# Decay matmuls on 128 partitions, every mask added on TensorE, and the y sum of the scan by one reduction over three planes

## The chip, the cores and the metric

The kernel runs on 1 core of one Trainium2 chip. The metric is the device time of one execution in microseconds (us), the median of the runs shown. Engine names as in the profile: PE is TensorE's matmul, PEld its weight load, DVE is VectorE, ACT ScalarE, POOL GpSimd, SP the engine whose queue issues every DMA of this kernel.

## The reference, cut to what matters

One step of a two-layer trunk over 256 context and 1024 latent tokens, width 1024. Layer one is attention beside a convolution. Layer two, which the change is about, is a bidirectional scan: 32 heads of 64 channels, 4 groups that share B and C, a state of 128, chunks of 128 tokens.

```python
a_cum = jnp.cumsum(dtc * a_neg.reshape(G, E), axis=2)
seg = a_cum[:, :, :, None] - a_cum[:, :, None, :]
decay = jnp.exp(jnp.where(causal, seg, -jnp.inf))
cb = jnp.einsum('bclgn,bcsgn->bclsg', cf, bf)
y_diag = jnp.einsum('bclsg,bclsge,bcsgep->bclgep', cb, decay, xdt)
...
y_off = jnp.einsum('bclgn,bcgepn,bclge->bclgep', cf, prev, jnp.exp(a_cum))
y = (y_diag + y_off).reshape(b, L, G, E, P)
...
y = y_f + jnp.flip(y_b, 1) + d_skip.reshape(SSD_GROUPS, SSD_HPG, 1) * xs
y = rmsnorm(y.reshape(b, L, SSD_INNER) * jax.nn.silu(z), g_norm)
```

## The kernel before, in words

Everything is held transposed, channels on the partitions and tokens along the row. Large products are done as three matmuls (`mm3`, lines 119 to 121: high by high, high by low, low by high part, in `F32R`), each moving 512 or 256 columns.

Layer two goes in 8 units `u` of 4 heads. For each unit the loop over the 10 chunks `c` of 128 tokens runs `scan_a(u, c + 1)` (one chunk ahead), then `scan_b(u, c)`, then `advance`, which carries the forward state. Between them a scheduler, which orders each engine's instructions ahead of time, lays the matmuls and convolutions of the next unit's input blocks (`conv_block`, `z_block`: lines 119 to 121 into `psmm`, line 848 on DVE), so that TensorE has long runs of dense matmuls around the scan's small ones. In the last unit, u = 7, no input blocks of a next unit are left.

`scan_a` makes the decay matrices of 4 heads and both directions (`dr`). A decay exponent is a difference of two running sums, one by row and one by column, and it is made by one matmul over 10 rows per direction: rows 0 and 1 of a group multiply ones by the high and low part of the one sum (tile `mv`, 4 heads by 128 columns), rows 2 to 9 multiply the other sum's parts (tile `lt`) by rows of `mv` that are one for one head and zero elsewhere. Direction 0 lies on partitions 0 to 9 and direction 1 on partitions 32 to 41 of the same two tiles (line 1136). Then the causal mask, 0 or -1e30, has to be added before the exponential. In the units below `MU = 6` DVE adds it (line 1141) and ACT takes the exponential of the sum in SBUF (line 1142). In units 6 and 7 a bf16 matmul of an identity with the mask adds it in PSUM (line 1144), and ACT reads PSUM (line 1145). POOL adds the two directions (line 1152) and DVE multiplies by `cb` (line 1153).

`scan_b` makes the output y of a chunk: `po` (line 1165) is the part of the states that come in, for one or both directions, and DVE multiplies it in place by the factors `eb`, planes [j, direction, t] (line 1174). `pd` (line 1170) is the part inside the chunk. Then DVE adds `pd` and the D term `xdv` (line 1178), adds the plane of each direction (line 1180, twice where there are two), and multiplies by the gate (line 1181). In chunks 0 and 1 only one direction has a state, so 8 of a unit's 10 chunks have two.

`load_m` brings 2 rows of `mv` and 8 of `lt` per direction (lines 1113 and 1114), two buffers each; `load_x` brings `xa`, 1024 columns of the array `cmb` (B, x, C, D term, gate), and the two halves of `eb`. All stand in SP's one queue.

Of the kernel before, what the change touches and what calls it, by code (L numbers as in the profile page):

```python
# [10 lines left out]
F32 = mybir.dt.float32  # L11
F32R = mybir.dt.float32r
I32 = mybir.dt.int32
BF16 = mybir.dt.bfloat16
AF = mybir.ActivationFunctionType
ALU = mybir.AluOpType
AX = mybir.AxisListType
# [39 lines left out]
def _body(nc, tc, d, es, dbg, stop):  # L57
    V, S, G, PE = nc.vector, nc.scalar, nc.gpsimd, nc.tensor
    dma = nc.sync.dma_start
# [11 lines left out]
    def f32(ap):  # L71
        return ap.bitcast(F32)
# [23 lines left out]
    ident = cp.tile([128, 128], F32, name="ident")  # L96
# [111 lines left out]
    sel = cp.tile([128, 2], F32, name="sel")  # L208
# [67 lines left out]
    def row(name="row", n=T, parts=128, dt=F32):  # L276
        return rows.tile([parts, n], dt, name=name, tag="row")
# [153 lines left out]
    fold = att.tile([64, 64], F32, name="fold", bufs=1)  # L431
    dma(fold, d["fold"])
    for c0, n in CHUNKS:
        ps = psum()
# [18 lines left out]
    for i in range(2):  # L453
        wh, wl = split_w(d["wa"][9 + i], 8, 128)
        s = row("qsq")
# [65 lines left out]
    for c0, n in CHUNKS:  # L521
        ps = bcast_cols(rq, c0 // 128, n // 128, ps=psum("pt"))
# [177 lines left out]
    for i in range(len(units) + 2):  # L700
        if i < len(units):
            u = units[i]
# [102 lines left out]
    cc = pool("cc", side="right", stack=esC)  # L805
# [11 lines left out]
    identb = cc.tile([128, 128], BF16, name="identb")  # L817
    V.tensor_copy(identb, ident)
    maskb = cc.tile([128, 2, 128], BF16, name="maskb")
    NMV, MU = 2, 6  # L820
    dec_bc = cc.tile([128, 128, 5], F32, name="dec_bc")
    dte = cc.tile([128, NCH, 2, NH], F32, name="dte")

    cmb = dp.tile([8, NCH, 128, 1408], F32, name="cmb")
    yzd = dp.tile([16, 128, T], F32, name="yzd")
    mvd = dp.tile([NCH, 2, 2, NH, 128], F32, name="mvd")
    ltd = dp.tile([NCH, 2, NH, 2, 128], F32, name="ltd")
# [30 lines left out]
        lin(wh, wl, 8, 128, h_h, h_l, CHUNKS, cb)  # L858
        return conv_post(blk, raw)

    OB, OX, OCT, OXD, OSZ, OBT = 0, 128, 384, 512, 768, 1024

    def z_part(blk, tz, w=None):
        wh, wl = w or split_w(d["wc"][blk], 8, 128)
# [48 lines left out]
    cr = pool("crow", bufs=4, side="left", stack=esK)  # L913
    maskU = cr.tile([128, 128], F32, name="maskU", tag="row")
    maskL = cr.tile([128, 128], F32, name="maskL", tag="row")
# [13 lines left out]
    w = dtile("w")  # L929
    S.activation(w, z, AF.Square)  # L930
    p = dtile("p")
# [43 lines left out]
    for half in range(2):  # L975
        hs = slice(half * 64, half * 64 + 64)
        for c0 in range(0, 5):
            c = half * 5 + c0
            ps = psum("sd")
# [20 lines left out]
            dma(eyd[half * 5:half * 5 + 5, :, dr].rearrange("c r t -> r c t"),  # L1000
                ey[r0:r0 + 32, :].rearrange("r (c t) -> r c t", t=Q))
    mvs, lts = [], []
    cts = [cr.tile([64, w], F32, name=n, tag="row") for n, w in (("mvc", 512), ("ltc", 128))]
    for t, n in zip(cts, ("mvc", "ltc")):
        dma(t, d[n])
    for i in range(NMV):
        mv = cc.tile([64, 512], F32R, name=f"mv{i}")
        lt = cc.tile([64, 128], F32R, name=f"lt{i}")
        S.copy(mv, cts[0])
        S.copy(lt, cts[1])  # L1010
        mvs.append(mv)
        lts.append(lt)
    dump("al", al)
# [43 lines left out]
    sp = pool("ssd", bufs=2, side="right", stack=esC)  # L1057
# [50 lines left out]
    xas, ebs, cbs, bts = {}, {}, {}, {}  # L1108

    def load_m(u, c):  # L1110
        mv, lt = mvs[c % NMV], lts[c % NMV]
        for dr in range(2):
            dma(f32(mv[32 * dr:32 * dr + 2]), mvd[c, dr, :, 4 * u:4 * u + 4].rearrange("x h t -> x (h t)"))
            dma(f32(lt[32 * dr + 2:32 * dr + 10]), ltd[c, dr, 4 * u:4 * u + 4].rearrange("h x t -> (h x) t"))

    def load_x(u, c):
        xa = xas[c] = sp.tile([128, 1024], F32, name="xa", tag="xa", bufs=3)
        dma(xa, cmb[u, c, :, 0:1024])
        if u % 2 == 0:
            bts[c] = sp.tile([128, 128], F32, name="bt", tag="bt")  # L1120
            dma(bts[c], cmb[u, c, :, OBT:OBT + 128])
        eb = ebs[c] = sp.tile([128, 2, 2, 128], F32, name="eb", tag="eb")
        for pr_ in range(2):
            ev = eyd[c, 4 * u:4 * u + 4].rearrange("(j p) d t -> p j (d t)", p=2)[pr_]
            dma(eb[pr_ * 64:pr_ * 64 + 64].rearrange("p j d t -> p j (d t)"),
                ev.unsqueeze(0).to_broadcast([64, 2, 256]))

    def scan_a(u, c):
        xa = xas[c]
        ct = xa[:, OCT:OCT + 128]  # L1130
        mv, lt = mvs[c % NMV], lts[c % NMV]
        pss = [psum("sd") for _ in range(2)]
        es_ = [sp.tile([128, 4, 128], F32, name="et", tag="et", bufs=4) for _ in range(2)]
        for dr, ps in enumerate(pss):
            r = slice(32 * dr, 32 * dr + 10)
            PE.matmul(ps, lt[r], mv[r], start=True, stop=u < MU)  # L1136
        for dr, ps in enumerate(pss):
            et = es_[dr].rearrange("p h t -> p (h t)")
            p3, mk = ps.rearrange("p (h t) -> p h t", h=4), maskb[:, dr:dr + 1].to_broadcast([128, 4, 128])
            if u < MU:  # L1140
                V.tensor_add(es_[dr], p3, mk)
                S.activation(et, et, AF.Exp)  # L1142
            else:
                PE.matmul(p3, identb, mk, start=False, stop=True)
                S.activation(et, ps, AF.Exp)
        if u % 2 == 0:
            pc_ = psum("sd")
            PE.matmul(pc_[:, :128], bts[c], ct, start=True, stop=True)
            cbs[c] = sp.tile([128, 128], F32, name="cb", tag="cb", bufs=NCH)
            S.copy(cbs[c], pc_[:, :128])  # L1150
        mt = es_[0]
        G.tensor_add(mt, es_[0], es_[1])  # L1152
        V.tensor_mul(mt, mt, cbs[c].unsqueeze(1).to_broadcast([128, 4, 128]))
        return xa, mt

    def scan_b(u, c, prev, st, y):
        xa, mt = st
        xt, ct = xa[:, OX:OX + 256], xa[:, OCT:OCT + 128]
        xdv, szv = xa[:, OXD:OXD + 256], xa[:, OSZ:OSZ + 256]
        eb = ebs[c]  # L1160
        dirs = [dr for dr in range(2) if prev[dr] is not None]
        po = psum("sd")
        for dr in dirs:
            for pi in range(2):
                PE.matmul(po[:, dr * 256 + pi * 128:dr * 256 + (pi + 1) * 128],  # L1165
                          prev[dr][:, pi * 128:(pi + 1) * 128], ct, start=True, stop=True)
        pd = psum("tm" if u == 7 else "sd")
        for j in range(4):
            b, pi = (j % 2) * 64, j // 2
            PE.matmul(pd[b:b + 64, pi * 128:(pi + 1) * 128], xt[:, j * 64:(j + 1) * 64], mt[:, j, :],  # L1170
                      start=True, stop=True)
        d0, d1 = dirs[0], dirs[-1] + 1
        yo = eb[:, :, d0:d1].rearrange("p j d t -> p d j t")
        V.tensor_mul(yo, po[:, d0 * 256:d1 * 256].rearrange("p (d j t) -> p d j t", j=2, t=128), yo)

        def v2(ap):
            return ap.rearrange("p (a t) -> p a t", a=2)
        V.tensor_add(y, v2(pd[:, :256]), v2(xdv))
        for dr in dirs:
            V.tensor_add(y, y, eb[:, :, dr])  # L1180
        V.tensor_mul(y, y, v2(szv))
        sq, ac = eb[:, :, d0], ysq[:, c * Q:c * Q + Q]
        S.activation(sq, y, AF.Square)
        if u:
            G.tensor_add(sq[:, 0], sq[:, 0], sq[:, 1])
            G.tensor_add(ac, ac, sq[:, 0])
        else:
            G.tensor_add(ac, sq[:, 0], sq[:, 1])
# [32 lines left out]
    for u in range(8):  # L1221
# [24 lines left out]
        for c in range(NCH):  # L1246
# [7 lines left out]
            if u < 7:  # L1254
                y = sp.tile([128, 2, 128], F32, name="yz", tag="yz")
            else:
                y = ylast[c // 5][:, :, (c % 5) * Q:(c % 5 + 1) * Q]
# [10 lines left out]
            elif c % 5 == 4:  # L1268
                f = c // 5
# [130 lines left out]
def _tables():  # L1400
    rows_ = TS // GRID_W
    f = np.float32
    r = np.repeat(np.arange(rows_, dtype=f), GRID_W)
    c = np.tile(np.arange(GRID_W, dtype=f), rows_)
    inv = np.power(f(10000.0), -np.arange(8, dtype=f) / f(8)).astype(f)
    ang = np.concatenate([r[:, None] * inv, c[:, None] * inv], axis=-1).astype(f)
    cos, sin = np.cos(ang).astype(f), np.sin(ang).astype(f)
    tab = np.zeros((128, T), f)
    tab[:96] = 1.0
    for i in range(32):  # L1410
        tab[64 + i, TP:] = cos[:, i // 2]
        tab[96 + i, TP:] = -sin[:, i // 2] if i % 2 == 0 else sin[:, i // 2]
    ident = np.eye(128, dtype=f)
    fold = np.zeros((64, 64), f)
    for i in range(64):
        for j in range(64):
            if i % 32 == j % 32:
                fold[i, j] = 1.0
    s, l = np.meshgrid(np.arange(128), np.arange(128), indexing="ij")
    maskU = (l >= s).astype(f)  # L1420
    maskL = (l <= s).astype(f)
    mvc = np.zeros((2, 32, 4, 128), f)
    ltc = np.zeros((2, 32, 128), f)
    ltc[:, 0:2] = 1.0
    for r in range(8):
        mvc[:, 2 + r, r // 2, :] = 1.0
    tab = np.stack([tab, np.concatenate([tab[64:], tab[:64]])])
    sel = np.zeros((128, 2), f)
    for i in range(128):
        if i % 32 < 2:  # L1430
            sel[i, i % 32] = 1.0
    return dict(sel=sel, tab=tab, ident=ident, fold=fold, maskU=maskU, maskL=maskL, mvc=mvc.reshape(64, 512), ltc=ltc.reshape(64, 128))


def _kblk(w):
# [107 lines left out]
```

## Time and profile before

| | |
|---|---|
| median of 3 runs | 2105.81 us (2104.4 to 2105.97) |
| profiled execution | 2106.15 us, of which the span from its first to its last instruction is 2104.3 us |
| busy in the span | PE 2024.6 us (96%), PEld 1627.3, DVE 1488.0 (71%), ACT 885.2 (42%), POOL 700.4 (33%) |
| mean granted TensorE clock | 0.981 |

Matmuls are pipelined: the duration of a matmul in the trace reaches past the start of the next one, and its end is modelled. What a matmul costs a busy PE is therefore read from the distance between two starts, and not from its duration, and PE may count as busy while it waits for weights. The scans of layer two lie from about 1090 us (the first decay matmul starts at 1093.8 us) to about 1895 us.

### The profile page before, as it was taken

Reading aid. Unit: us, or ns where it says so; the run is one execution under the profiler, and the core shown is the slowest. Engines: PE = TensorE matmul, PEld = TensorE weight load, DVE = VectorE, ACT = ScalarE, POOL = GpSimd, SP = SyncE. Lnnn points to the kernel's source line nnn. Section 1 sums busy time; section 2 is a strip of 40 time slices with the busy share of each in tenths; the row PEclk is TensorE's granted clock in tenths of the full one; section 3 lists DMA queues with packets and bytes.
Section 4 is the critical chain, followed back from the end, with each engine's and each line's share of the span. In section 5 each row is a group of like instructions: output and inputs, shape, how many; then the busy total and the mean of one; then the engine's idle time right before and its main releaser. Section 6 shows DMA issues by size and latency. Waiting matters only on the chain.

```text
span 2104.3 us, 32156 instructions
## 1 busy us (share of the span) xinstructions
PE 2024.6 (96%) x11710; PEld 1627.3 (77%) x11710; DVE 1488.0 (71%) x2361; ACT 885.2 (42%) x1683; POOL 700.4 (33%) x567
## 2 busy tenths in 40 slices
PE   6999999999999999989999999999999999899997
PEld 4777888677767768878887777778777777579997
DVE  5797897666666673457669797977898596873743
ACT  5411312566566672334544333343344333334531
POOL 1211112213141303543135354545454454662001
PEclk9999999999999999999999999999999999999998
DMA  8424123221112126222667657755765578655442
GB/s 331 165 105 147 53 103 121 63 75 43 54 46 76 51 83 220 108 86 76 176 205 220 207 176 211 215 169 187 222 198 181 166 218 252 215 173 191 143 154 70
DMA packets 251453, 313.32 MB, mean 149 GB/s; under 512 B 19904, under 2 KB 200096, under 8 KB 251296
## 3 DMA queue, kind: packets, MB, share of 16 engines
q1 hardware_dynamic: 251296, 311.28, 46.3%
q8 instruction: 93, 1.52, 0.3%
q14 instruction: 64, 0.52, 0.1%
HBM read 223.15 MB, written 88.05 MB: 148 GB/s over the span
## 4 chain that ended last, share of the span: by engine, by line
PE 79%; DVE 8%; DMA 4%; issue 3%; POOL 3%; ACT 1%; SPq 1%; DVEq 0%; POOLq 0%; ACTq 0%
PE psmm L119 16%; PE psmm L120 16%; PE psmm L121 16%; PE pspo L666 5%; PE pspt L646 4%; PE pss L119 3%; PE pssd L1078 2%; PE pss L120 2%; PE pss L121 2%; PE pssd L1165 2%; PE pssd L1136 2%; PE pssd L1170 1%; PE psx L229 1%; DVE cy L848 1%; DMA eb<-eyd 1%
## 5 line engine op out<-in xcount | busy, mean ns | idle before, releaser
L119 PE MATMUL psmm<-hl,wh 128*128 128x512 f32 (+1 forms) x1152 | 425.8, 370 | 7.0 <-ACT wh L114 3.5
L121 PE MATMUL psmm<-hl,wl 128*128 128x512 f32 (+1 forms) x1152 | 425.8, 370 | 4.0 <-POOL wl L115 4.0
L120 PE MATMUL psmm<-hl,wh 128*128 128x512 f32 (+1 forms) x1152 | 424.8, 369 | 0.0
L115 POOL TENSOR_TENSOR wl<-ws,wh 128x1024 fp32r<-128x1024 f32 x89 | 226.2, 2543 | 473.6 <-ACT wh L114 394.5
L119 PEld LDWEIGHTS psmm<-hl,wh 128*128 128x128 f32 x1152 | 222.6, 193 | 47.2 <-issue 9.5
L121 PEld LDWEIGHTS psmm<-hl,wl 128*128 128x128 f32 x1152 | 222.3, 193 | 41.0 <-issue 6.6
L120 PEld LDWEIGHTS psmm<-hl,wh 128*128 128x128 f32 x1152 | 222.7, 193 | 36.9 <-issue 8.3
L383 DVE SCALAR_TENSOR_TENSOR cacc<-cvin,acw,cacc 128x1295 f32<-128x1295 f32 x120 | 207.0, 1741 | 4.6 <-ACT cacc L378 3.1
L114 ACT CAST wh<-ws 128x1024 fp32r<-128x1024 f32 x109 | 113.5, 1042 | 196.1 <-PE psmm L120 136.7
L848 DVE SCALAR_TENSOR_TENSOR cy<-raw,prm,cy 128x1282 f32<-128x1282 f32 x96 | 164.8, 1717 | 20.8 <-ACT cy L845 19.7
L120 PE MATMUL psmm<-hlo,wh 128*128 128x512 f32 (+3 forms) x480 | 171.5, 358 | 0.1
L121 PE MATMUL psmm<-hh,wl 128*128 128x512 f32 (+3 forms) x480 | 169.3, 356 | 0.0
L119 PE MATMUL psmm<-hh,wh 128*128 128x512 f32 (+3 forms) x480 | 167.6, 359 | 1.6 <-ACT hh L259 1.6
L617 DVE TENSOR_REDUCE mx<-pss 128x1 f32<-128x512 f32 (+1 forms) x208 | 137.3, 668 | 35.4 <-PE pss L121 34.6
L1152 POOL TENSOR_TENSOR et<-et 128x512 f32<-128x512 f32 x80 | 118.9, 1486 | 104.9 <-ACT et L1142 75.7
L120 PE MATMUL psmm<-yl,wh 128*128 128x256 f32 (+1 forms) x476 | 148.3, 313 | 2.7 <-DVE yl L1208 2.7
L119 PE MATMUL psmm<-yh,wh 128*128 128x256 f32 (+1 forms) x476 | 148.2, 315 | 0.3 <-ACT yh L1207 0.2
L121 PE MATMUL psmm<-yh,wl 128*128 128x256 f32 (+1 forms) x476 | 147.7, 314 | 0.0
L626 ACT ACTIVATE prob<-pss,nm 128x512 f32<-128x512 f32 x192 | 130.3, 693 | 16.1 <-DVE nm L621 14.2
L1083 POOL TENSOR_TENSOR st<-st,dec_bc 128x256 f32<-128x256 f32 x104 | 86.2, 834 | 130.5 <-DVE st L1085 79.2
L646 PE MATMUL pspt<-ident,prob 128*128 128x128 f32 x800 | 122.2, 279 | 4.6 <-ACT prob L626 3.7
L652 ACT COPY ptile<-pspt 128x512 f32<-128x512 f32 (+1 forms) x144 | 81.3, 569 | 105.8 <-PE pspt L646 105.0
(336 smaller groups left out, 4204.3 us busy)
## 6 DMA issues: line engine op xcount, KB each, us to landing
xa<-cmb SPq DMA_DIRECT2D x80, 512.0 KB
wm<-in_wmod_dram SPq DMA_DIRECT2D x48, 512.0 KB
ws<-in_wc_dram SPq DMA_DIRECT2D x40, 512.0 KB
eb<-eyd SPq DMA_DIRECT2D x160, 128.0 KB
ws<-in_wco_dram SPq DMA_DIRECT2D x32, 512.0 KB
cmb<-xt SPq DMA_DIRECT2D x24, 640.0 KB
bx<-cmb SPq DMA_DIRECT2D x72, 192.0 KB
ws<-in_wa_dram SPq DMA_DIRECT2D x19, 512.0 KB
```

The costliest lines, as they stand in the source:

```text
L114: S.copy(wh, ws)
L115: (eng or G).tensor_sub(wl, ws, f32(wh))
L119: PE.matmul(ps, lh, rh, start=start, stop=False)
L120: PE.matmul(ps, lh, rl, start=False, stop=False)
L121: PE.matmul(ps, ll, rh, start=False, stop=stop_)
L383: V.scalar_tensor_tensor(cacc[i], cv[:, k:k + CO], acw[:, 31 * i + k:31 * i + k + 1], cacc[i], ALU.mult, ALU.add)
L617: V.tensor_reduce(mx[:, x:x + 1], ps[:, :n], axis=AX.X, op=ALU.max, negate=len(segs) == 1)
L626: S.activation(prob[:, c:c + n], ps[:, :n], AF.Exp, bias=nm, accum_out=sums[:, x:x + 1])
L646: PE.transpose(ps[:, x * 128:(x + 1) * 128], prob[:, (g + x) * 128:(g + x + 1) * 128], ident)
L666: PE.matmul(po[64 * j:64 * j + 64, 0:256], vt[:, kt, 64 * h:64 * h + 64], pts[(j, 4 * (x // 4))][:, x % 4, :], start=x == 0, stop=x == len ...
L848: V.scalar_tensor_tensor(y, raw[:, k:k + RO], ccw[:, 5 * blk + k:5 * blk + k + 1], y, ALU.mult, ALU.add)
L1152: G.tensor_add(mt, es_[0], es_[1])
```

## The change

Three things are changed. First, `mv` and `lt` get 128 partitions. `lt` gets a plane for each direction, zero in all rows but the direction's own ten, and each decay matmul runs over all 128 partitions, with `lt[:, dr]` as weights and the whole of `mv` moving. Second, `MU` is gone: in every unit the mask is added by the bf16 matmul on TensorE, and the exponential reads PSUM. Third, the D term is not loaded with `xa` (now 768 columns) but by a DMA of its own into a third plane of `eb`; where there are two directions one `tensor_reduce` sums the three planes into y, elsewhere one `tensor_add` sums the two that are there, and `pd` is added last.

```diff
-    NMV, MU = 2, 6
+    NMV = 2
...
-    OB, OX, OCT, OXD, OSZ, OBT = 0, 128, 384, 512, 768, 1024
+    OB, OX, OCT, OSZ, OXD, OBT = 0, 128, 384, 512, 768, 1024
...
-        mv = cc.tile([64, 512], F32R, name=f"mv{i}")
-        lt = cc.tile([64, 128], F32R, name=f"lt{i}")
+        mv = cc.tile([128, 512], F32R, name=f"mv{i}")
+        lt = cc.tile([128, 2, 128], F32R, name=f"lt{i}")
...
-            dma(f32(lt[32 * dr + 2:32 * dr + 10]), ltd[c, dr, 4 * u:4 * u + 4].rearrange("h x t -> (h x) t"))
+            dma(f32(lt[32 * dr + 2:32 * dr + 10, dr]), ltd[c, dr, 4 * u:4 * u + 4].rearrange("h x t -> (h x) t"))
...
-        xa = xas[c] = sp.tile([128, 1024], F32, name="xa", tag="xa", bufs=3)
-        dma(xa, cmb[u, c, :, 0:1024])
+        xa = xas[c] = sp.tile([128, OXD], F32, name="xa", tag="xa", bufs=3)
+        dma(xa, cmb[u, c, :, 0:OXD])
...
-        eb = ebs[c] = sp.tile([128, 2, 2, 128], F32, name="eb", tag="eb")
+        eb = ebs[c] = sp.tile([128, 2, 3, 128], F32, name="eb", tag="eb")
+        dma(eb[:, :, 2], cmb[u, c, :, OXD:OXD + 256].rearrange("p (j t) -> p j t", j=2))
...
-            r = slice(32 * dr, 32 * dr + 10)
-            PE.matmul(ps, lt[r], mv[r], start=True, stop=u < MU)
+            PE.matmul(ps, lt[:, dr], mv, start=True, stop=False)
...
-            if u < MU:
-                V.tensor_add(es_[dr], p3, mk)
-                S.activation(et, et, AF.Exp)
-            else:
-                PE.matmul(p3, identb, mk, start=False, stop=True)
-                S.activation(et, ps, AF.Exp)
+            PE.matmul(p3, identb, mk, start=False, stop=True)
+            S.activation(et, ps, AF.Exp)
...
-        V.tensor_add(y, v2(pd[:, :256]), v2(xdv))
-        for dr in dirs:
-            V.tensor_add(y, y, eb[:, :, dr])
+        if len(dirs) == 2:
+            V.tensor_reduce(y, eb.rearrange("p j d t -> p j t d"), axis=AX.X, op=ALU.add)
+        else:
+            V.tensor_add(y, eb[:, :, d0], eb[:, :, 2])
+        V.tensor_add(y, v2(pd[:, :256]), y)
         V.tensor_mul(y, y, v2(szv))
...
-    mvc = np.zeros((2, 32, 4, 128), f)
-    ltc = np.zeros((2, 32, 128), f)
-    ltc[:, 0:2] = 1.0
+    mvc = np.zeros((4, 32, 4, 128), f)
+    ltc = np.zeros((4, 32, 2, 128), f)
+    for dr in range(2):
+        ltc[dr, 0:2, dr] = 1.0
     for r in range(8):
-        mvc[:, 2 + r, r // 2, :] = 1.0
+        mvc[0:2, 2 + r, r // 2, :] = 1.0
```

The scheduler orders the changed kernel anew. On TensorE, where unit 2 ends and unit 3 begins, these rows stood before (line 1136 is a decay matmul, lines 119 to 121 the dense matmuls of the next unit's input blocks, lines 1165 and 1170 `po` and `pd`):

```order
L119 MATMUL psmm<-hl,wh 128x512
L120 MATMUL psmm<-hl,wh 128x512
L1136 MATMUL pssd<-mv_9073,lt_9074 128x512
L121 MATMUL psmm<-hl,wl 128x512
L1136 MATMUL pssd<-mv_9073,lt_9074 128x512
L1165 MATMUL pssd<-xa,st 128x128 x2
```

and these in the changed kernel (its line 1140 is the mask's weight load and matmul, its lines 1161 and 1166 are `po` and `pd`):

```order
L120 MATMUL psmm<-hl,wh 128x256
L121 MATMUL psmm<-hl,wl 128x256
L1136 MATMUL pssd<-mv_9073,lt_9074 128x512
L1140 LDWEIGHTS identb
L1140 MATMUL pssd<-maskb,identb 128x512
L119 MATMUL psmm<-hl,wh 128x256
L120 MATMUL psmm<-hl,wh 128x256
L1136 MATMUL pssd<-mv_9073,lt_9074 128x512
L1140 LDWEIGHTS identb
L1140 MATMUL pssd<-maskb,identb 128x512
L1161 MATMUL pssd<-xa,st 128x128 x2
L1166 MATMUL pssd<-et,xa 64x128 x4
```

The decay matmuls keep their places between dense ones, and a mask matmul now stands right behind each. On DVE, in the middle of the scans, the sum of y stood like this (lines 1174, 1178, 1180 twice, 1181, with the state's lines 1085 and 1075 between them):

```order
L1174 TENSOR_TENSOR eb<-pssd,eb 128x2x2x128
L1178 TENSOR_TENSOR yz<-pssd,xa 128x256
L1180 TENSOR_TENSOR yz<-yz,eb 128x256
L1085 TENSOR_TENSOR st<-st,pssd 128x256
L1075 TENSOR_TENSOR xw<-xa,dte 128x256
L1180 TENSOR_TENSOR yz<-yz,eb 128x256
L1085 TENSOR_TENSOR st<-st,pssd 128x256
L1181 TENSOR_TENSOR yz<-yz,xa 128x256
```

and in the changed kernel like this (its lines 1170, 1175, 1178 and 1179 in the same roles; line 848 is a convolution tap of the next unit):

```order
L1170 TENSOR_TENSOR eb<-pssd,eb 128x2x2x128
L1175 TENSOR_REDUCE yz<-eb 128x256
L848 SCALAR_TENSOR_TENSOR cy<-raw_8583,prm,cy 128x1282
L1178 TENSOR_TENSOR yz<-pssd,yz 128x256
L1149 TENSOR_TENSOR et<-et,cb 128x512
L848 SCALAR_TENSOR_TENSOR cy<-raw_8583,prm,cy 128x1282
L1085 TENSOR_TENSOR st<-st,pssd 128x256
L1075 TENSOR_TENSOR xw<-xa,dte 128x256
L1179 TENSOR_TENSOR yz<-yz,xa 128x256
```

The reduction stands where the first sum stood and needs only `eb`; `pd` is needed one operation later.

## Rows read from the trace of the kernel before

**Rows 1.** The page: busy time of PE; the chain that ended last, by engine.

```profile
PE 2024.6 (96%) x11710; PEld 1627.3 (77%) x11710; DVE 1488.0 (71%) x2361; ACT 885.2 (42%) x1683; POOL 700.4 (33%) x567
...
PE 79%; DVE 8%; DMA 4%; issue 3%; POOL 3%; ACT 1%; SPq 1%; DVEq 0%; POOLq 0%; ACTq 0%
```

**Rows 2.** Stretches: length; PE, PEld, DVE, ACT, POOL busy; granted clock; DMA.

```profile
1040.00:1740.00 700.00, 683.86 (x3756) 543.01 (x3755) 564.03 (x825) 274.43 (x459) 326.55 (x305) 0.98 0.65 196
1740.00:1905.00 165.00, 151.57 (x928) 119.06 (x927) 121.21 (x201) 59.91 (x115) 93.41 (x96) 0.97 0.66 210
1905.00:2104.00 199.00, 187.21 (x1276) 186.59 (x1274) 104.21 (x196) 73.93 (x121) 17.55 (x14) 0.96 0.41 139
```

**Rows 3.** Eight stretches of the scans at a low clock: one, and their sum.

```profile
1157.00:1164.00 7.00, 6.13 (x30) 5.62 (x31) 6.90 (x13) 3.83 (x9) 2.50 (x3) 0.51 0.75 221
...
sum 37.60, PE 35.42 PEld 30.37 DVE 31.17 ACT 12.05 POOL 17.07; mean PE 4.43 PEld 3.80 DVE 3.90 ACT 1.51 POOL 2.13
```

**Rows 4.** PE and PEld in order of time, dense matmuls: start us, duration us, instruction.

```profile
1301.62 0.39 PE L119 MATMUL psmm<-hl,wh 128*128 128x512 f32 x1
1301.84 0.39 PE L120 MATMUL psmm<-hl,wh 128*128 128x512 f32 x1
1301.85 0.19 PEld L121 LDWEIGHTS psmm<-hl,wl 128*128 128x128 f32 x1
...
1311.14 0.28 PE L120 MATMUL psmm<-hl,wh 128*128 128x256 f32 x1
```

**Rows 5.** The same view around two decay matmuls apart, and two together (x2).

```profile
1302.84 0.50 PE L1136 MATMUL pssd<-mv,lt 10*128 10x512 f32 x2
1303.26 0.50 PE L120 MATMUL psmm<-hl,wh 128*128 128x512 f32 x1
...
1311.26 0.28 PE L121 MATMUL psmm<-hl,wl 128*128 128x256 f32 x1
1311.47 0.49 PE L1136 MATMUL pssd<-mv,lt 10*128 10x512 f32 x1
1311.89 0.38 PE L119 MATMUL psmm<-hl,wh 128*128 128x256 f32 x1
1312.20 0.50 PE L1136 MATMUL pssd<-mv,lt 10*128 10x512 f32 x1
```

**Rows 6.** Waits of the weight load, 1040 to 1738 us: total us, times, longest.

```profile
PEld psmm L120 <- issue: 8.1, 34, 0.2
```

**Rows 7.** Around masks on TensorE in the last unit, in order of time.

```profile
1756.24 0.10 PEld L1144 LDWEIGHTS <-identb 128*128 128x128 bf16 x1 [0.24 <-issue]
...
1762.97 0.39 PE L1144 MATMUL pssd<-maskb,identb 128*128 128x512 bf16 x1
...
1763.32 0.28 PE L119 MATMUL psmm<-hl,wh 128*128 128x256 f32 x1
```

**Rows 8.** DVE groups by form: busy us, mean ns; then single groups: ns min/median/max.

```profile
L1180 DVE TENSOR_TENSOR yz<-yz,eb 128x256 f32<-128x256 f32 x126 | 87.0, 690 | 1.1
L1141 DVE TENSOR_TENSOR et<-pssd,maskb 128x512 f32<-128x512 f32 x120 | 79.9, 680 | 8.4 <-PE pssd L1136 7.9
...
L1180 DVE TENSOR_TENSOR yz<-yz,eb x126: 407/532/2211, 1107.2 to 1825.5; 128x256 f32<-128x256 f32 x126
...
L617 DVE TENSOR_REDUCE mx<-pss x208: 411/691/694, 380.1 to 784.1; 128x1 f32<-128x512 f32 x96, 128x1 f32<-128x256 f32 x8
```

**Rows 9.** A stall of PE in unit 0, all engines in order of time.

```profile
1154.42 2.52 POOL L115 TENSOR_TENSOR wl<-ws,wh 128x1024 fp32r<-128x1024 f32 x1
...
1154.77 2.45 DVE L1181 TENSOR_TENSOR yz<-yz,xa 128x256 f32<-128x256 f32 x1
...
1157.87 0.91 PE L1170 MATMUL pssd<-et,xa 128*64 128x128 f32 x6 [2.65 <-DVE et L1141]
```

**Rows 10.** SP's queue in order of time, and DVE's waits for the `eb` load, 1040 to 1738 us.

```profile
1304.31 1.24 SPq L1125 DMA_DIRECT2D eb<-eyd  x2
...
DVE eb L1174 <- DMA eb<-eyd: 7.1, 5, 3.3
```

More of the change, by code (lines that the diff above doesn't have):

```diff
@@ L1002, in _body @@
     mvs, lts = [], []
-    cts = [cr.tile([64, w], F32, name=n, tag="row") for n, w in (("mvc", 512), ("ltc", 128))]
+    cts = [cr.tile([128, w], F32, name=n, tag="row") for n, w in (("mvc", 512), ("ltc", 256))]
     for t, n in zip(cts, ("mvc", "ltc")):
@@ L1006, in _body @@
     for i in range(NMV):
-        mv = cc.tile([64, 512], F32R, name=f"mv{i}")
-        lt = cc.tile([64, 128], F32R, name=f"lt{i}")
+        mv = cc.tile([128, 512], F32R, name=f"mv{i}")
+        lt = cc.tile([128, 2, 128], F32R, name=f"lt{i}")
         S.copy(mv, cts[0])
-        S.copy(lt, cts[1])
+        S.copy(lt.rearrange("p d s -> p (d s)"), cts[1])
         mvs.append(mv)
@@ L1121, in load_x @@
             dma(bts[c], cmb[u, c, :, OBT:OBT + 128])
-        eb = ebs[c] = sp.tile([128, 2, 2, 128], F32, name="eb", tag="eb")
+        eb = ebs[c] = sp.tile([128, 2, 3, 128], F32, name="eb", tag="eb")
+        dma(eb[:, :, 2], cmb[u, c, :, OXD:OXD + 256].rearrange("p (j t) -> p j t", j=2))
         for pr_ in range(2):
             ev = eyd[c, 4 * u:4 * u + 4].rearrange("(j p) d t -> p j (d t)", p=2)[pr_]
-            dma(eb[pr_ * 64:pr_ * 64 + 64].rearrange("p j d t -> p j (d t)"),
+            dma(eb[pr_ * 64:pr_ * 64 + 64, :, 0:2].rearrange("p j d t -> p j (d t)"),
                 ev.unsqueeze(0).to_broadcast([64, 2, 256]))
@@ L1158, in scan_b @@
         xt, ct = xa[:, OX:OX + 256], xa[:, OCT:OCT + 128]
-        xdv, szv = xa[:, OXD:OXD + 256], xa[:, OSZ:OSZ + 256]
+        szv = xa[:, OSZ:OSZ + 256]
         eb = ebs[c]
@@ L1431, in _tables @@
             sel[i, i % 32] = 1.0
-    return dict(sel=sel, tab=tab, ident=ident, fold=fold, maskU=maskU, maskL=maskL, mvc=mvc.reshape(64, 512), ltc=ltc.reshape(64, 128))
+    return dict(sel=sel, tab=tab, ident=ident, fold=fold, maskU=maskU, maskL=maskL, mvc=mvc.reshape(128, 512), ltc=ltc.reshape(128, 256))
 def _kblk(w):
```

## The prediction

> **What bounds the kernel now.** I read the page first: PE is busy for 96% of the span, and 79% of the chain that ended last is PE [rows 1]. So PE time saved or added counts, and time on another engine counts only where PE waits for it. The busy times by stretch confirm this for the part that the change touches: from 1040 to 1740 us PE is idle for 700 - 683.9 = 16.1 us, from 1740 to 1905 us for 165 - 151.6 = 13.4 us, while DVE is busy for 564.0 and 121.2 us of them [rows 2]. DVE is close behind and can make PE wait. The same view over eight short stretches shows the clock: for 37.6 us of the scans the granted clock was 0.5 of full speed, the 1.2 GHz level [rows 3]. Work done there would have taken half, so this costs up to 18.8 us.
>
> A busy PE may still be waiting, so I then read starts of matmuls in order of time. Dense matmuls start 0.22 to 0.23 us apart at 512 columns (1301.62, 1301.84) and 0.12 apart at 256 (1311.14 to 1311.26), and a weight load (1301.85) runs beside the matmul before its own [rows 4, 5]. Around a decay matmul that stops. The dense matmul of 1311.26 should release PE at 1311.38, yet the decay matmul starts at 1311.47: 0.09 late. The next dense matmul starts 0.42 after it, with no weight load running beside it. That one, of 256 columns, takes 0.31 to the next start: 0.12 of its own, 0.09 ahead of the next decay matmul, and 0.10 more. One decay matmul alone thus takes 0.09 + 0.42 + 0.10 = 0.61 us of PE. Two together (the x2 of 1302.84) start together and also give way after 0.42 [rows 5]. The waits name the same thing: the dense weight loads sat idle for 8.1 us in 34 cases of about 0.24 us, released by nothing but "issue", and the two other lines of the three have the like, 96 cases in all [rows 6].
>
> **Part one, 128 partitions.** The decay matmul now has the shape of the dense ones, 128 by 128 weights and 512 columns of the same type, so I give it their distance, 0.23. I counted places in the order of the instructions before: below unit 6 there are 90 decay matmuls alone, 13 places of two and one of four; in units 6 and 7, 32 alone with their mask behind them, and 4 places of two.
> - Alone: 0.61 - 0.23 = 0.38 saved, times 90 = 34 us.
> - Two together: 0.61 against 0.46, 0.15 saved, times 15 = 2 us.
> - Alone with a mask behind: the mask's weight load is late too (0.24 idle ahead of it, and 0.10 long [rows 7]), but nothing is late behind the mask, so I leave out the 0.10: 0.09 + 0.42 - 0.23 = 0.28, times 32 = 9 us. Its 4 places of two give nearly nothing.
>
> Together 45 us of PE.
>
> The Trainium skill speaks against this part: "TensorE: Matmul & The Clock Gate", section "Why this matters for your kernels", has a matmul of 32 rows take as long as one of 128, and counsels slices on separate row groups so that they run at once. By that rule the 106 or so matmuls alone would gain nothing, and each of 19 pairs would lose its overlap. The trace agrees on the overlap (two start together in rows 5), but not on the rest: 0.42 at 10 rows against 0.23 at 128.
>
> **Part two, the masks.** Ahead of the scheduler's choice stands the sum: 120 more mask matmuls. In unit 7 one starts at 1762.97; behind it come one dense matmul of 256 columns and the next start at 1763.32 [rows 7]. That is 0.35, less 0.12: 0.23 us a mask, with no loss behind it. 120 x 0.23 = 28 us more on PE. What no row shows is a mask behind a 128-row matmul: each mask before stood behind a 10-row one, and its weight load waited 0.24. Low bound: nothing more than 0.23, since weights of 128 rows load beside a running matmul everywhere else [rows 4]. High bound: the 0.24 stays, for 160 masks 38 us. I take the low bound: the same wait stands behind 10-row matmuls whatever comes next, masks or dense [rows 6, 7], so it belongs to the 10-row one.
>
> DVE loses 79.9 us of mask sums [rows 8]. The exponential now waits for ACT with the PSUM bank still taken, where DVE used to free it; units 6 and 7 already do this.
>
> **Part three, the sum of y.** Two sums of a plane, 0.69 us each on average, become one reduction over 768 elements. By the reductions of line 617, 0.41 at 256 and 0.69 at 512 elements, it takes 0.97 [rows 8]. So 64 chunks save 1.38 - 0.97 = 0.41 us each, 26 us of DVE. The plane stride of the reduction is shown by no row; were it slowed as the sums are beside POOL (0.407 alone, 0.690 on average), it would take 1.65 and DVE would lose 17 us, still far less than the masks free. In the other 16 chunks a sum replaces a sum. In total DVE gets some 106 us freer out of 685 [rows 2], and `pd` is now followed by two operations instead of four.
>
> The D term costs one more DMA a chunk in SP's queue. The two `eb` loads take 1.24 us to issue [rows 10], so 0.6 each, 80 x 0.6 = 48 us of a queue over 800 us. `eb` lands 0.6 later where it was already late, 5 waits of line 1174: 3 us at most. Also each decay matmul now needs the rows of both directions, later by at most one such issue at 8 unit starts: 5 us at most. Both loads stand a chunk or two ahead of their use, so I price them at nothing, with 8 us as the bound.
>
> **What follows from a freer DVE.** The pot is the idle PE, 29.5 us, and the clock, 18.8 us. One row shows how they hang together: a POOL subtraction of 2.52 us ran beside the gate product of line 1181, which took 2.45 where sums of that size take 0.41 alone [rows 8]; the masks of the next chunk queued behind it on DVE, `pd` waited 2.65 us for them, and the low-clock stretch of 1157 us followed [rows 3, 9]. With the masks on PE the exponential no longer waits for that queue, though line 1153's product still does. Other stalls wait for DMA or stand at unit ends. I take 11 us of the 48; the bounds are nothing and 35 (all but the part that DMA ends).
>
> **The sum.** Against the profiled execution, 2106.15 us (span 2104.3 and 1.85 around it; the median of the runs is 2105.81, the same within 0.02%): -45 + 28 - 11 = -28 us, 2078 us. A chance of 0.5, with a range of its own from 2063 to 2092.
>
> **Rivals.**
> - *The freer DVE gives much more.* PE's stalls and low-clock stretches mostly go: -45 + 28 - 35 = -52, 2054 us. For it: the stall of rows 9. Against it: DMA share 0.65 in the same stretch [rows 2], which stays. Chance 0.15.
> - *It gives nothing,* or the new order puts as many stalls in other places: -17, or with the 8 us of later loads -9: 2089 to 2097. For it: all of PE's order behind 1090 us is laid anew. Chance 0.17.
> - *Slower: the weight loads stay late.* If what holds them is not the 10 rows but the change between unlike matmuls, each mask behind its decay matmul still costs 0.24 (38 us), or the decay matmul keeps its 0.61. The first gives 2078 + 38 = 2116. The second loses the 45 and keeps the 28 and the 11: 2123 us. It decides from 28 / 160 = 0.18 us a place. By the skill's rule (rows do not matter, and the pairs lose their overlap) the time would be about 2127, with 19 pairs times 0.23 on top; the trace speaks against it by 0.42 to 0.23. For it: the mask has never stood behind a wide decay matmul. Against it: `po` and dense matmuls of different kinds follow each other with no such wait. Chance 0.13.
> - *Neither:* savings and masks cancel within 0.2%, which is about what a measurement of this kernel can tell. Chance 0.05.
>
> **How the numbers follow.** Faster by over 0.2%: 0.5 + 0.15 + 0.17 = 0.82. Within 0.2%: 0.05. Slower: 0.13. The range leaves out the slower rival and the far end of the first one: 2048 to 2101 us.
>
> **What would show it.** The starts around a decay matmul in the dense stretch: 0.23 apart, and no weight load idle by "issue" behind it; 160 masks at 0.22 to 0.23 between starts. DVE's line for the masks gone, the reduction near 0.97 us, DVE's busy time down by about 100 us. Fewer and shorter low-clock stretches between 1090 and 1900 us. The forecast is wrong if weight loads behind decay matmuls or masks still sit idle for 0.24 us, if the reduction takes over 1.4 us, if PE waits for the exponential with all PSUM banks taken, or if new stalls of over a microsecond stand where the old ones were.

## The result, and the profile after

The changed kernel takes 2084.68 us (median of 4 runs, 2081.21 to 2086.83) against 2105.11 us (4 runs): ratio 0.9900, 95% interval 0.9888 to 0.9912, 20 us faster. The forecast was 2078 us, 28 us faster. The sum of the terms was near; what the three parts are worth one by one turned out to be quite different, as the experiments show.

The page of the profile after, span and busy times, answering to [rows 1]:

```profile
span 2083.3 us, 32430 instructions
...
PE 1999.5 (96%) x11830; PEld 1629.6 (78%) x11830; DVE 1391.4 (67%) x2177; ACT 876.8 (42%) x1683; POOL 707.3 (34%) x567
```

PE has 120 instructions more and is busy for 25 us less; DVE is busy for 97 us less. The busy times by stretch (length; PE, PEld, DVE, ACT, POOL; granted clock; DMA), as in [rows 2]:

```profile
1040.00:1740.00 700.00, 690.08 (x4022) 564.49 (x4020) 489.05 (x684) 277.83 (x480) 344.81 (x318) 1.00 0.69 205
1740.00:1905.00 165.00, 142.56 (x916) 121.89 (x915) 107.14 (x176) 56.20 (x103) 88.58 (x87) 0.94 0.65 205
```

In units 0 to 5 (unit 6 starts at 1737.8 us before and at 1709.7 now) PE is now idle for 9.9 us instead of 16.1, and the granted clock is 1.00 all the time. In the last units PE is idle for 22.4 us instead of 13.4 and the clock still falls. All low-clock stretches of the scans together, as in [rows 3] (one, and the sum of four):

```profile
1778.00:1784.80 6.80, 4.09 (x13) 3.06 (x14) 3.03 (x7) 1.66 (x4) 2.81 (x5) 0.50 0.52 159
...
sum 20.40, PE 16.74 PEld 13.91 DVE 13.07 ACT 7.33 POOL 7.47; mean PE 4.19 PEld 3.48 DVE 3.27 ACT 1.83 POOL 1.87
```

20.4 us at half speed instead of 37.6. PE in order of time around a decay matmul and its mask, answering to [rows 4, 5, 7]:

```profile
1325.77 0.39 PE L120 MATMUL psmm<-hl,wh 128*128 128x512 f32 x1
1326.00 0.39 PE L1136 MATMUL pssd<-mv,lt 128*128 128x512 f32 x1
1326.23 0.39 PE L1140 MATMUL pssd<-maskb,identb 128*128 128x512 bf16 x1
1326.27 0.58 PE L121 MATMUL psmm<-hl,wl 128*128 128x512 f32 x1
1326.68 0.39 PE L119 MATMUL psmm<-hl,wh 128*128 128x512 f32 x1
1326.91 0.40 PE L120 MATMUL psmm<-hl,wh 128*128 128x512 f32 x1
```

The decay matmul starts 0.23 after the dense one, the mask 0.23 after that, and from the mask to the start at 1326.68, with one dense matmul of 0.23 between, it is 0.45: 0.22 for the mask. (The start shown for the dense matmul right behind the mask, 0.04 after it, is not a distance to build on; the one after it makes up for it.) The place costs 0.46 us, where a decay matmul without a mask cost 0.61.

The waits of PE and of its weight load, 1040 to 1740 us, longest first, as in [rows 6]:

```profile
PEld L1140 <- issue: 25.9, 114, 0.3
PEld pssd L1136 <- DVE eb L1170: 5.8, 4, 2.0
```

The long waits of the dense weight loads behind a decay matmul are gone. The mask's own weight load still sits idle for 0.23 us in 114 cases, which the forecast had named as a sign that it was wrong. It isn't one: the starts are 0.23 apart all the same. This load takes 0.10 us, and no start shows a loss to it. The DVE groups that answer to [rows 8] (the first line is from the kernel before, where the product by `cb` is line 1153), and the reductions into `yz` one by one, as ns min/median/max:

```profile
L1153 DVE TENSOR_TENSOR et<-et,cb 128x512 f32<-128x512 f32 x80 | 68.5, 858 | 21.3 <-POOL et L1152 21.1 <-ACT cb L1150 0.2
...
L1149 DVE TENSOR_TENSOR et<-et,cb 128x512 f32<-128x512 f32 x80 | 67.1, 839 | 51.3 <-POOL et L1148 47.3 <-ACT cb L1146 4.0
L1175 DVE TENSOR_REDUCE yz<-eb 128x256 f32<-128x768 f32 x56 | 57.9, 1034 | 0.9
...
L1175 DVE TENSOR_REDUCE yz<-eb x56: 1020/1033/1051, 1127.5 to 1799.4; 128x256 f32<-128x768 f32 x56
```

The reduction takes 1.03 us (0.97 was forecast). Ahead of the product by `cb` DVE now waits 47.3 us for POOL's sum of the directions, where it waited 21.1 us before. And all 56 of these reductions take 1.02 to 1.05 us, though 30 of them run beside POOL for 0.2 us or more. The sums of a plane that they replace took 0.41 to 0.43 us alone and up to 2.56 (median 0.84) beside POOL.

### The profile page after: what moved, and what is told of

Its sections match the earlier page's. It is cut to its first block, busy times and chain, and to the rows that moved or that the text cites. A ratio compares the mean times of both kernels' runs of the same rounds, so it can differ in the third digit from the quotient of the medians.

```text
span 2083.3 us, 32430 instructions
## 1 busy us (share of the span) xinstructions
PE 1999.5 (96%) x11830; PEld 1629.6 (78%) x11830; DVE 1391.4 (67%) x2177; ACT 876.8 (42%) x1683; POOL 707.3 (34%) x567
## 5 line engine op out<-in xcount | busy, mean ns | idle before, releaser
L119 PEld LDWEIGHTS psmm<-hl,wh 128*128 128x128 f32 x1152 | 219.0, 190 | 35.9 <-ACT wh L114 4.3
L120 PEld LDWEIGHTS psmm<-hl,wh 128*128 128x128 f32 x1152 | 219.0, 190 | 30.1 <-issue 1.2
L1148 POOL TENSOR_TENSOR et<-et 128x512 f32<-128x512 f32 x80 | 125.1, 1564 | 72.1 <-ACT et L1141 69.7
L626 ACT ACTIVATE prob<-pss,nm 128x512 f32<-128x512 f32 x192 | 130.2, 693 | 16.1 <-DVE nm L621 14.2
```

Source lines behind the costliest of these rows:

```text
L119: PE.matmul(ps, lh, rh, start=start, stop=False)
L120: PE.matmul(ps, lh, rl, start=False, stop=False)
L626: S.activation(prob[:, c:c + n], ps[:, :n], AF.Exp, bias=nm, accum_out=sums[:, x:x + 1])
```

## The experiments

Each ran (4 to 10 runs) on one chip with runs of the kernel before, whose medians there were 2105.59 to 2106.19 us. Most of them switch the three parts of the change on and off. In what follows "excess" is worked out from the trace: over all PE matmuls from 1060 us to the last `pd`, the distance to the next start less what the columns take in a dense row (0.227 us at 512, 0.119 at 256, 0.111 at 128, 0.216 for a mask, 0.055 for a `pd` of half width, 0.213 for a state matmul of 256). Distances of over 0.6 us excess are counted as gaps, and everything at the low clock apart from both. The trace is of one execution: for rows alone it took 6 us more than the median, for the sum alone 4 us more, for the masks left out 6 us less, so their gaps can be off by as much. Before: 82 us of small excess, 30 of gaps, 18 at the low clock. After: 42, 34 and 8, and 26 us more of columns (120 masks x 0.216).

### Rows alone

```diff
-            r = slice(32 * dr, 32 * dr + 10)
-            PE.matmul(ps, lt[r], mv[r], start=True, stop=u < MU)
+            PE.matmul(ps, lt[:, dr], mv, start=True, stop=u < MU)
```

with the tiles `mv` and `lt` of 128 partitions; all else as before.

> The change's first part alone: decay matmuls over 128 partitions, masks and the sum of y as before. Theory A (PE's own time decides: a decay matmul alone cost about 0.62 us of PE and costs 0.23 on 128 partitions): 40 us of PE less and nothing added, stalls and low-clock stretches about as before; 2062 to 2075 us, faster than the change itself. Theory B (what counted was the relief of DVE, and the rows are worth little): DVE is as loaded as before, so 2098 to 2106 us. Starts: 0.23 from a decay matmul to the next one under A, 0.42 under B.

Measured: 2107.21 us, ratio 1.0015 (0.9999 to 1.0032). No gain at all, though PE did save what was forecast. PE in order of time:

```profile
1308.40 0.28 PE L121 MATMUL psmm<-hl,wl 128*128 128x256 f32 x1
1308.52 0.40 PE L1135 MATMUL pssd<-mv,lt 128*128 128x512 f32 x1
1308.76 0.28 PE L119 MATMUL psmm<-hl,wh 128*128 128x256 f32 x1
1308.87 0.40 PE L1135 MATMUL pssd<-mv,lt 128*128 128x512 f32 x1
1309.11 0.28 PE L120 MATMUL psmm<-hl,wh 128*128 128x256 f32 x1
```

Each decay matmul takes 0.24 or less, and the small excess falls from 82 to 44 us. But the gaps grow from 30 to 63 us and the low clock from 18 to 27. The stretch of units 0 to 5 and the waits of PE there say for whom:

```profile
1040.00:1740.00 700.00, 658.13 (x3768) 551.45 (x3767) 572.52 (x826) 273.85 (x460) 325.48 (x304) 0.98 0.66 197
...
PE pssd L1169 <- DVE et L1140: 9.3, 6, 2.6
PE pssd L1078 <- DVE et L1140: 6.1, 8, 2.1
```

PE is idle for 41.9 us instead of 16.1, and what it waits for most is DVE's mask sum (line 1140 there): 18.4 us of these, where the same waits (on line 1141) came to 5.8 us before. The time that PE gained went into waiting, for DVE above all. Theory A, that PE's own time decides, falls in that form; theory B's time is nearer (1 us above its range), but the rows are not worth little to PE, as it had it.

### Masks alone

```diff
-    NMV, MU = 2, 6
+    NMV, MU = 2, 0
```

> The second part alone: every mask on TensorE, decay matmuls on 10 rows, the sum as before. Theory A: a decay matmul and its mask alone take about 0.8 us where the decay matmul took 0.63, so 17 to 28 us more of PE over 120 masks, less some 5 to 10 us of stalls: 2113 to 2125 us, slower. Theory B (relief of DVE pays): 80 us less of DVE shorten stalls and low-clock stretches by 15 us or more than the masks cost: 2085 to 2095 us.

Measured: 2104.50 us, ratio 0.9987 (0.9978 to 0.9997). Neither theory: a place with its mask takes 0.75 us (median), PE's columns and small excess together grow by 22 us, the gaps and the low clock shrink from 48 to 24 us (DVE is busy for 478 of 700 us instead of 564), and the two nearly cancel.

### Sum alone

Only the third part: the D term in the third plane of `eb`, the reduction, `pd` added last.

> The third part alone: D term in a plane of eb, the reduction, pd added last; decay matmuls and masks as before. Theory A: PE's own work is the same and DVE is not the bound, so within 0.3% of before, 2098 to 2106 us; the reduction takes 0.95 to 1.0 us and DVE is busy for some 25 us less. Theory B: the shorter way from pd to y shortens stalls; 2085 to 2095 us.

Measured: 2091.48 us, ratio 0.9917 (0.9900 to 0.9935). Of the three parts this is the only one that gains by itself, 15 us. The small excess is as before (86 us), and the gain lies in the gaps and the low clock, 48 to 30 us. Units 0 to 5:

```profile
1040.00:1740.00 700.00, 696.65 (x3874) 550.08 (x3873) 549.75 (x793) 281.34 (x473) 328.73 (x313) 1.00 0.69 205
```

PE is idle for 3.4 us and the clock stays at 1.00. So a part that takes nothing from PE gained the most. Theory B has the time right; the reason that it gives, the shorter way from `pd` to y, is tried next.

### Order of the sum alone

```diff
-        V.tensor_add(y, v2(pd[:, :256]), v2(xdv))
-        for dr in dirs:
+        V.tensor_add(y, v2(xdv), eb[:, :, d0])
+        for dr in dirs[1:]:
             V.tensor_add(y, y, eb[:, :, dr])
+        V.tensor_add(y, v2(pd[:, :256]), y)
```

> The kernel before with one edit: the sum of y begins with the D term and the planes of eb and adds pd last; still three sums, nothing else changed. If the gain of the third part alone (14.7 us) came from DVE's shorter way from pd to y, most of it shows here: 2088 to 2096 us. If it came from the reduction's 26 us less of DVE, or from the D term's own DMA, the time stays within 4 us of before: 2101 to 2109 us.

Measured: 2107.75 us, ratio 1.0008 (0.9987 to 1.0028). The shorter way from `pd` to y is not the cause. What stays is the reduction (less DVE time, and a time that does not grow beside POOL), the D term's own DMA, which makes the `xa` load a quarter smaller, or the order that the scheduler lays for this kernel; no run tells these apart.

### Pairs of parts

Rows and sum (masks as before), rows and masks (sum as before), and masks and sum (decay matmuls on 10 rows).

> The change without its second part: 128 partitions and the reduction, masks below unit 6 on DVE as before. Theory A: PE saves 40 us and pays for no masks, so 2055 to 2070 us, 15 us or more under the changed kernel's 2085. Theory B: with 80 us of masks back on DVE the stalls and low-clock stretches come back, 2085 to 2100 us, no better than the changed kernel.

> Parts one and two, the sum of y as before. Theory C (PE and DVE are both near their limit): PE is 14 us less busy than before as in the changed kernel, and DVE 80 us less, so most of the gain is there without the reduction: 2083 to 2094 us. If the reduction is what the gain needs (it helped alone where 80 us of masks did not): 2096 to 2106 us.

> Parts two and three with the decay matmuls on 10 rows. Theory C: DVE is relieved by both, so PE alone decides; each of 160 places takes 0.75 us instead of 0.46, about 40 us less the overlap of pairs, and the time is 2100 to 2118 us, slower than the third part alone (2091). If DVE's relief adds up: 2080 to 2092 us.

Measured, with all eight cases side by side (medians, ratio to the kernel before in the same job, interval):

| parts | us | ratio | interval |
|---|---|---|---|
| none | 2105 to 2106 | 1 | |
| rows | 2107.21 | 1.0015 | 0.9999 to 1.0032 |
| masks | 2104.50 | 0.9987 | 0.9978 to 0.9997 |
| sum | 2091.48 | 0.9917 | 0.9900 to 0.9935 |
| rows, masks | 2098.09 | 0.9963 | 0.9951 to 0.9975 |
| rows, sum | 2083.67 | 0.9889 | 0.9874 to 0.9904 |
| masks, sum | 2095.47 | 0.9951 | 0.9936 to 0.9966 |
| all three | 2084.68 | 0.9900 | 0.9888 to 0.9912 |

The parts don't add. The rows gain nothing alone (their interval includes 1) and 0.2 to 0.5% beside any other part. Four pairs of kernels differ in the rows alone, and in each PE's small excess falls by 32 to 41 us while its gaps and its low clock together grow: by 42 us with nothing else changed, 28 beside the masks, 33 beside the sum, 22 beside both. So most of the PE time that the rows save comes back as waits, and the less of it the more the other parts relieve DVE (26 us by the sum, 80 by the masks, 106 by both, as forecast). The masks on TensorE gain 0.5% beside the rows alone (DVE was what PE waited for), lose 0.3% beside the sum alone, and do nothing beside rows and sum. The full change is no faster than rows and sum without the masks: their intervals overlap. For rows and sum theory B's 2085 to 2100 us was nearer than A's 2055 to 2070. For masks and sum the relief of DVE did not add up (2080 to 2092), nor was it as slow as theory C had it. Rows and masks came out in the range of 2096 to 2106 us, which held that the gain needs the reduction, and not in theory C's.

### Masks left out

```diff
-            PE.matmul(ps, lt[:, dr], mv, start=True, stop=False)
+            PE.matmul(ps, lt[:, dr], mv, start=True, stop=True)
...
-            PE.matmul(p3, identb, mk, start=False, stop=True)
-            S.activation(et, ps, AF.Exp)
+            S.activation(et, ps, AF.Exp, scale=0.0)
```

> The changed kernel with the masks left out on both engines (no mask matmul, no mask sum; the exponential is taken with scale 0, so its values are all one and the output is not the reference's). Theory C (PE and DVE are both near their limit in the scans, so that 40 us saved on PE alone come back as waits for DVE, and both have to be relieved): with neither 28 us of masks on PE nor 80 us on DVE the time falls by 15 to 30 us below the changed kernel, 2055 to 2070 us, with few stalls of PE over 0.6 us. Theory D (what bounds the scans now is something else, DMA or the chain from chunk to chunk): the time stays within 8 us of the changed kernel, 2077 to 2090 us.

Measured: 2068.02 us, ratio 0.9822 (0.9801 to 0.9844). With the masks on neither engine the time falls 17 us under the changed kernel, within what theory C gave. But theory C's sign, few stalls of PE over 0.6 us, does not show: there are 26 such gaps with 38 us, against 21 with 34 us in the changed kernel. In the longest PE waits for DVE's lines 1085 and 1075 (up to 3.4 and 5.4 us), so the masks are not all that holds PE up, and what else does was not switched off. The masks cost about the same 16 us whether TensorE adds all 160 (35 us of its columns) or DVE adds the 120 of units 0 to 5 (80 us of DVE) and TensorE the rest.

### Masks twice

```diff
+            PE.matmul(p3, identb, mk, start=False, stop=False)
             PE.matmul(p3, identb, mk, start=False, stop=True)
```

> The changed kernel with each mask added twice on TensorE (the masked entries become -2e30, the result is the same): 160 more mask matmuls of 0.22 to 0.23 us, 36 us of PE, with nothing changed on DVE. If PE's own time sets the end (theory A, and C with DVE now relieved): 2110 to 2122 us. If PE has slack against DVE or DMA (theory D): less than half of it, 2085 to 2102 us.

Measured: 2109.59 us, ratio 1.0020 (1.0008 to 1.0031): 25 us above the changed kernel, for 35 us of PE (160 x 0.216; a place goes from 0.46 to 0.68 us, median). Some 70% of added PE time reaches the end. The rest is covered: gaps and the low clock shrink from 42 to 25 us. It lies below the range of A and C, and above the half that D allowed.

### 64 rows

```diff
-            PE.matmul(ps, lt[:, dr], mv, start=True, stop=False)
+            PE.matmul(ps, lt[0:64, dr], mv[0:64], start=True, stop=False)
```

> The changed kernel with the decay matmuls on partitions 0 to 63 instead of 0 to 127 (rows 64 to 127 hold zeros and are left out). If it is the full height of the array that lets the next weights load beside the matmul (theory A on the mechanism), the 0.42 us to the next start and the 0.24 us idle weight load come back: about 0.75 to 0.8 us for a decay matmul and its mask instead of 0.46, 30 to 45 us more of PE, 2105 to 2130 us. If 64 rows are enough, or if what counted was that both directions share one set of rows, 0.46 stays and the time is 2080 to 2090 us.

Measured: 2104.90 us, ratio 0.9998 (0.9983 to 1.0013), 20 us slower than at 128. PE in order of time:

```profile
1310.37 0.40 PE L119 MATMUL psmm<-hl,wh 128*128 128x512 f32 x1
1310.69 0.50 PE L1136 MATMUL pssd<-mv,lt 64*128 64x512 f32 x1
1311.13 0.39 PE L1140 MATMUL pssd<-maskb,identb 128*128 128x512 bf16 x1
1311.17 0.59 PE L120 MATMUL psmm<-hl,wh 128*128 128x512 f32 x1
1311.59 0.40 PE L121 MATMUL psmm<-hl,wl 128*128 128x512 f32 x1
```

The weight load of the decay matmul, in the changed kernel (the matmul starts at 1326.00) and here (it starts at 1310.69):

```profile
1325.77 0.19 PEld L1136 LDWEIGHTS pssd<-mv,lt 128*128 128x128 f32 x1
...
1310.69 0.18 PEld L1136 LDWEIGHTS pssd<-mv,lt 64*128 64x128 f32 x1 [0.36 <-issue]
```

The decay matmul is 0.09 late again and the mask starts 0.44 after it, as at 10 rows; the place takes 0.75 us (median), and the small excess is 36 us larger than in the changed kernel. At 128 rows the weights load beside the matmul before, 0.23 ahead of their own; at 64 their load stands idle until the matmul itself starts. The edit changes nothing but the number of rows, so 128 rows let the load run beside the neighbour and 64 do not. No run lies between the two, and since the neighbours have 128 rows in every run, none tells whether full height counts or the same height as the neighbours.

### Sharing the masks

Two tries at a better version, with DVE adding some masks as before and TensorE the others: by unit (`MU = 3` in the changed kernel), and by direction in units 0 to 5 (`u < MU and dr == 0` on DVE, with `MU = 6`).

> The changed kernel with DVE adding the masks in units 0 to 2 and TensorE in units 3 to 7. All masks on TensorE and the masks of six units on DVE took the same time (2085 and 2084 us). Theory C: if both loads stall the scans, half of each gives less of either, 2074 to 2082 us. If each mask costs the same on either engine: 2081 to 2087 us.

> The changed kernel with DVE adding the masks of direction 0 and TensorE those of direction 1 in units 0 to 5, so that the load of each chunk is halved on both engines. Theory C: 2072 to 2081 us, under both kernels. If each mask costs the same on either engine: 2081 to 2087 us.

Measured: by unit 2090.19 us, ratio 0.9921 (0.9904 to 0.9937), outside both ranges; by direction 2081.10 us, ratio 0.9883 (0.9859 to 0.9908), at the border of its two ranges. The second has the lowest median of all complete kernels, but its interval overlaps that of the change and of rows and sum, so none is shown to be the best.

## Why the prediction was right, and where its steps were not

The price of the rows and of the masks on PE came out as forecast, and that is most of the sum. That the total fell so near is partly luck, though: by the same terms rows and sum without the masks would have come at about 2061 us (an estimate, 2106 less 45), and they measured 2083.67, 23 us later.

- **The price of a decay matmul: right.** 0.46 us for a decay matmul and its mask, as forecast (0.23 and 0.23). The rows took 40 us of small excess off PE (82 to 42; 45 forecast), the masks added 26 (28 forecast). The net of PE is -14 us against -17. (By the counts of part one, 90 and 32, the matmuls that stand alone are 122 and not 106 or so; no sum uses the 106.)
- **The slower rival: wrong, and shown so.** No wait stays at the masks' weights that costs PE anything, and the 64-row run shows a height at which the wait is back.
- **"PE time saved or added counts, and time on another engine counts only where PE waits for it": this step failed as it was used.** It led me to book 45 us of PE as a gain in its own right, and all the relief of DVE as a by-product of 11 us. Rows alone saved that PE time and gained nothing, because PE then waited, longest for DVE's masks; the sum alone left PE's work as it was and gained 15 us. In the scans a term taken from PE is worth its length only as long as what feeds PE keeps pace: the four pairs that differ in the rows show it, with 22 to 42 us of new waits for 32 to 41 us saved. That it is DVE alone that has to keep pace is not shown, since with the masks on neither engine the waits stay. The row that could have warned of it was there: DVE busy 564 of 700 us beside PE's 684 [rows 2], with a mask sum in DVE's queue ahead of what PE waited for in the one stall shown [rows 9].
- **What a freer DVE gives: too large in the sum, and the place is another.** 11 us were forecast; gaps and low clock went from 48 to 42 us, 6 less. In units 0 to 5 it did more than forecast (29 to 11 us, and the clock is never low there), but in the last units new gaps took most of it back (19 to 31 us). The longest stand in unit 6; the rows there, and after them the same product in the kernel with the sum alone:

```profile
1775.60 0.70 PE L1078 MATMUL pssd<-xw,xa 128*128 128x256 f32 x2
...
1780.18 0.42 DVE L1075 TENSOR_TENSOR xw<-bx,dte 128x256 f32<-128x256 f32 x1 [0.30 <-DMA bx<-cmb]
1780.71 1.19 PE L1078 MATMUL pssd<-xw,bx 128*128 128x256 f32 x2 [4.41 <-DVE xw L1075]
...
1786.62 1.19 PE L1078 MATMUL pssd<-xw,bx 128*128 128x256 f32 x2 [4.23 <-DVE xw L1075]
```

PE waits 4.41 us for a product whose operand `bx` had just landed, and the low-clock stretch of 1778 us begins in that wait. The forecast had left such waits for DMA outside its bound for the gain, but not that there would be more of them. They come with the third part: the kernel with the sum alone has the same two waits (8.4 us from 1700 to 1860 us, 8.5 in the changed kernel), and the kernel before has none for `xw` there. `bx` is late because its load is issued late, at 1776.13 us and 4.05 us ahead of its use, where the nine loads of `bx` over unit 6 before were issued 5.7 to 23.1 us ahead. Whether the added DMA pushes it back in SP's queue or the new order alone does was not tried.
- **The D term's DMA: under-priced.** I allowed `eb` 3 us more of late landing, and priced it at nothing in the sum. DVE's waits for it from 1040 to 1740 us went from 7.1 us in 5 cases to 11.9 us in 3 (`DVE eb L1170 <- DMA eb<-eyd: 11.9, 3, 5.3` in the waits after), and from 1740 to 1905 us from 3.0 to 9.9 us. Some of it reaches PE: its waits for the line of DVE that needs `eb`, ahead of a decay matmul, grew from 1.4 to 7.6 us between 1060 and 1900 us. How much of this is the D term's DMA and how much the new order, no run shows.
- **The reduction: nearly right** in its length (1.03 for 0.97 us, so 22 us of DVE saved instead of 26). That it, or the D term's DMA that comes with it, would be the one part that gains alone was not foreseen.

The time came out 7 us above the forecast: PE's net is 3 us smaller and the stalls gave 6 us instead of 11.

## What to carry to other kernels

Where two engines are both busy for most of a stretch and feed each other (here 98% and 81%), a saving on one is not a gain to be added up: try it alone and with the other engine relieved, and look at what its waits become. Between dense matmuls of 128 rows, a matmul of 10 or 64 rows was dear by the weight loads around it; padded with zero rows to 128 it cost 0.23 us like its neighbours. Moving work between two such engines can be worth nothing in either direction.

## What the hardware showed that I had not expected

A matmul of 64 rows behaves between dense ones like one of 10 (0.44 and 0.42 us to the next start), not like one of 128 (0.23). An idle weight load need not cost anything: the masks' loads sit idle for 0.23 us in 114 places and the matmuls' starts show no loss. And the reduction over three planes kept its time beside POOL (1.02 to 1.05 us in all 56 cases), where the sums of two tiles that it replaced went from 0.41 up to 2.56 us.
